# RMSNorm with ReLU on one core: twelve transfers instead of seventeen, and constant addresses on VectorE and ScalarE

## The chip, the core and the metric

The kernel runs on one core of a Trainium2 chip. A core has five engines. Three of them matter here: ScalarE (ACT in the profile) and VectorE (DVE) compute, and SyncE (SP) issues the transfers between main memory (HBM) and the on-chip memory (SBUF, 128 partitions). GpSimd (POOL) only passes semaphores on. TensorE is idle. The transfers themselves are done by 16 DMA engines, each with its own queue. The metric is the device time of one execution in microseconds (us); the time of the kernel before is 160.51 us, the median of three runs that lie between 160.47 and 160.72.

## The reference

```python
def reference(x, gamma, eps):          # x: 16 x 1024 x 512 float32
    rms = np.sqrt(np.mean(x ** 2, axis=-1, keepdims=True) + eps)
    x_norm = x / rms * gamma
    return np.maximum(x_norm, 0).astype(np.float32)
```

Each of the 16,384 rows of 512 numbers is divided by its own root mean square, multiplied by `gamma`, and clamped at zero. The input is 33.55 MB and so is the output, so 67.1 MB pass through the DMA engines whatever the program does.

## The kernel before

**Tiling.** Each partition holds 128 rows in all. They are cut into eight chunks of K = 16 rows (4 MB over all partitions), and each chunk into two groups of G = 8 rows. SBUF has room for six chunks at a time: `slots` is one tensor of six slots, and chunk i lives in slot i % 6. In HBM a chunk is one block of 4 MB in which every partition owns 16 consecutive rows, 32 KB. All computing is done in place in `slots`.

**Transfers.** All are issued by SP, in one written order, and each DMA engine works its queue in that order. There are 17: chunk 0 is loaded in two halves (lines 59 and 77), the others whole, and each of the eight chunks is stored whole (line 87). The two halves are issued ahead of Tile's closing barrier (`tc.close()`, line 97), everything else behind it. The loads of chunks 1 to 5 follow at once. Then SP waits:

```python
    nc.sync.wait_ge(tick3, 6)
    store(0)
    store(1)
    for s in range(2):
        nc.sync.wait_ge(sem_slot[s], 32)
        load(7 + s)
    nc.sync.wait_ge(tick1, 11)
    for i in range(2, nchunks):
        store(i)
```

`tick3` reaches 6 when VectorE has done three rows of group 5 (chunk 2, row 10), `tick1` reaches 11 with the first row of group 10. `load(7 + s)` is chunk 6 + s, which goes into the slot that store s has emptied. Each store also waits until its own chunk is done (`done`).

**ScalarE** (lines 131 to 143) runs a loop over the 16 groups. When GpSimd has told it that a group is there (`ready`), it squares and sums each of the 8 rows (line 136: one ACTIVATE and one read of the accumulator), then takes the root over the 8 sums (line 142) and raises `sq`. **VectorE** (lines 147 to 167) runs a loop over the same groups: a reciprocal of the 8 roots (line 152), one SCALAR_TENSOR_TENSOR for each row that multiplies by the reciprocal and by `gamma` (line 157), and one TENSOR_SCALAR that clamps the whole group, 128x4096 (line 167). Both loops compute the address of each row in a register while they run: ahead of each row's instruction stands a register instruction (FUSED_REGOPS).

**Start.** VectorE clears `gseed` and `eps_sb` (lines 122, 123); ScalarE waits for that, loads `gamma` into four partitions of `gseed` (line 126), and VectorE spreads it over all partitions (line 146).

Of the kernel before, what the change touches and what calls it, by code (L numbers as in the profile page):

```python
# [1 line left out]

# [4 lines left out]

F32 = mybir.dt.float32
ALU = mybir.AluOpType
ACTF = mybir.ActivationFunctionType  # L10


@with_exitstack
def kernel(
    ctx: ExitStack,
    tc: tile.TileContext,
    x: bass.AP,
    gamma: bass.AP,
    eps: bass.AP,
    out: bass.AP,  # L20
):

    nc = tc.nc
    P = nc.NUM_PARTITIONS

    x2 = x.flatten_outer_dims()
    out2 = out.flatten_outer_dims()  # L30
    n, d = x2.shape
    rows = n // P
    inv_d = 1.0 / d
    K = 16
    G = 8
    nchunks = rows // K
    nslots = 6
    ngroups = rows // G
    per = K // G
    xv = x2.rearrange("(c p k) d -> c p k d", p=P, k=K)  # L40
    ov = out2.rearrange("(c p k) d -> c p k d", p=P, k=K)

    def sbuf(name, shape):
        return nc.alloc_sbuf_tensor(name, shape, F32).ap()

    gseed = sbuf("gseed", [P, d])
    gamma_sb = sbuf("gamma_sb", [P, d])
    eps_sb = sbuf("eps_sb", [P, 1])
    ss = sbuf("ss", [P, rows])
    rms = sbuf("rms", [P, rows])  # L50
    rstd = sbuf("rstd", [P, rows])
    slots = sbuf("slots", [P, nslots * K * d])
    junk = nc.alloc_psum_tensor("junk", [P, G, d], F32).ap()


    loads = [(0, 0, G), (0, G, K - G)] + [(i, 0, K) for i in range(1, nchunks)]


    sem_half = nc.alloc_semaphore("half")
    sem_slot = [nc.alloc_semaphore(f"slot{s}") for s in range(nslots)]  # L60
    sem_g = nc.alloc_semaphore("gam")
    sem_z = nc.alloc_semaphore("zero")
    ready = nc.alloc_semaphore("ready")
    sq = nc.alloc_semaphore("sq")
    tick1 = nc.alloc_semaphore("tick1")
    tick3 = nc.alloc_semaphore("tick3")
    done = nc.alloc_semaphore("done")
    sa = nc.alloc_semaphore("sa")
    sv = nc.alloc_semaphore("sv")

    def slot_ap(i):
        s = (i % nslots) * K * d
        return slots[:, s:s + K * d].rearrange("p (k d) -> p k d", d=d)

    def load(m):
        i, a, r = loads[m]
        return nc.sync.dma_start(out=slot_ap(i)[:, a:a + r, :],
                                 in_=xv[i][:, a:a + r, :]
                                 ).then_inc(sem_half if m == 0 else sem_slot[i % nslots], 16)

    def take(engine, sem, n):
        engine.wait_ge(sem, n)
        engine.sem_inc(sem, -n)  # L83

    def store(i):
        nc.sync.wait_ge(done, per * (i + 1))
        nc.sync.dma_start(out=ov[i], in_=slot_ap(i)).then_inc(sem_slot[i % nslots], 16)

    ctx.enter_context(tc.manual_schedule(engines={mybir.EngineType.SP}))
    early = 2
    for m in range(early):
        t = load(m)
        tc.no_tile_sem_insts.add(t.ins.name)
    ctx.close()
    tc.close()
    tc.compile()  # L98

    for m, (i, a, r) in enumerate(loads):  # L100
        if m >= early and i < nslots:
            load(m)


    nc.sync.wait_ge(tick3, 6)
    store(0)
    store(1)
    for s in range(2):
        nc.sync.wait_ge(sem_slot[s], 32)
        load(7 + s)  # L110
    nc.sync.wait_ge(tick1, 11)
    for i in range(2, nchunks):
        store(i)

    for m, (i, a, r) in enumerate(loads):
        if m == 0:
            take(nc.gpsimd, sem_half, 16)
        else:
            nc.gpsimd.wait_ge(sem_slot[i % nslots], 32 * (i // nslots) + 16)
        nc.gpsimd.sem_inc(ready, r // G)  # L120

    nc.vector.memset(gseed, 0.0).then_inc(sem_z, 1)  # L122
    nc.vector.memset(eps_sb, eps).then_inc(sem_z, 1)  # L123

    nc.scalar.wait_ge(sem_z, 1)
    nc.scalar.dma_start(out=gseed[0:P:32, :],
                        in_=gamma[None, :].to_broadcast([P // 32, d])
                        ).then_inc(sem_g, 16)
    nc.scalar.preload_act_table(ACTF.Sqrt)  # L129
    take(nc.scalar, sem_z, 2)  # L130
    with nc.scalar.Fori(0, ngroups) as gi:
        take(nc.scalar, ready, 1)
        base = nc.scalar.snap((gi % (nslots * per)) * (G * d))
        col = nc.scalar.snap(gi * G)
        for j in range(G):
            a = nc.scalar.activation(  # L136
                out=junk[:, j, :], in_=slots[:, bass.ds(base + j * d, d)],
                func=ACTF.Square, accum_out=ss[:, bass.ds(col + j, 1)])
            if j == G - 1:
                a.then_inc(sa, 1)  # L140
        take(nc.scalar, sa, 1)
        nc.scalar.activation(out=rms[:, bass.ds(col, G)], in_=ss[:, bass.ds(col, G)],  # L142
                             func=ACTF.Sqrt, bias=eps_sb, scale=inv_d).then_inc(sq, 1)

    take(nc.vector, sem_g, 16)
    nc.vector.stream_shuffle(gamma_sb, gseed, [0] * 32)  # L146
    with nc.vector.Fori(0, ngroups) as gi:
        take(nc.vector, sq, 1)
        base = nc.vector.snap((gi % (nslots * per)) * (G * d))
        col = nc.vector.snap(gi * G)  # L150
        blk = slots[:, bass.ds(base, G * d)]
        nc.vector.reciprocal(out=rstd[:, bass.ds(col, G)],  # L152
                             in_=rms[:, bass.ds(col, G)]).then_inc(sv, 1)
        take(nc.vector, sv, 1)
        for j in range(G):
            row = slots[:, bass.ds(base + j * d, d)]
            r = nc.vector.scalar_tensor_tensor(  # L157
                out=row, in0=row, scalar=rstd[:, bass.ds(col + j, 1)], in1=gamma_sb,
                op0=ALU.mult, op1=ALU.mult)
            if j == 0:  # L160
                r.then_inc(tick1, 1)
            if j == 2:
                r.then_inc(tick3, 1)
            if j == G - 1:
                r.then_inc(sv, 1)
        take(nc.vector, sv, 1)
        nc.vector.tensor_scalar_max(out=blk, in0=blk, scalar1=0.0).then_inc(done, 1)  # L167

    take(nc.sync, done, ngroups)
    take(nc.sync, tick1, ngroups)  # L170
    take(nc.sync, tick3, ngroups)
    for i in range(nchunks - nslots, nchunks):
        take(nc.sync, sem_slot[i % nslots], 32 * (i // nslots + 1))


# [1 line left out]
_INS = ['x', 'gamma', 'eps']  # L177
_OUTS = [((16, 1024, 512), 'float32')]

_NUMBERS = {'eps': 9.999999747378752e-06}  # L180


# [26 lines left out]
```

## Time and profile before

| what | value |
|---|---|
| median of three runs | 160.51 us (160.47 to 160.72) |
| the profiled execution: its own time | 160.59 us |
| its span, first to last instruction | 159.3 us |
| DMA packets' time, share of 16 engines over the span | 98.2% |
| moved | 67.12 MB, mean 421 GB/s |
| VectorE busy | 126.0 us (79%) |
| ScalarE busy | 86.3 us (54%) |

The span is measured inside the program; 1.3 us of the execution's own time lie outside it. "Busy" counts an engine's compute instructions; register, branch and semaphore instructions are not in it. The DMA share is the time that the packets of a queue took, over 16 engines and the whole span. A packet here is what one DMA engine moves for one partition of one transfer; beside the data packets each engine writes the transfer's semaphore once, as a packet of 4 bytes.

### The profile page before, as it was taken

To read this page: it belongs to the slowest core of one execution; us is meant where nothing else is said; L and a number is where in the kernel's file an instruction comes from. 1 tells how busy PE (TensorE), PEld (TensorE's weight loads), DVE (VectorE), ACT (ScalarE), POOL (GpSimd) and SP (SyncE) were. 2 spreads that over 40 slices of the span, in tenths; PEclk is the share of its full clock that TensorE was granted. 3 is DMA by queue.
4 is the path that set the end of the run, shared out by engine and by line. 5 is a ranking of instruction groups with operands and counts; after the bars stand their busy time and mean duration, and the time that the engine had idled before them with its cause. 6 is when DMAs were issued, how large, how long until landed. Compare 5 with 4: busy or idle time off the path is not lost. (4 is left out here: it accounts for less than half of the span.)

```text
span 159.3 us, 999 instructions
## 1 busy us (share of the span) xinstructions
DVE 126.0 (79%) x164; ACT 86.3 (54%) x273; POOL 0.2 (0%) x4
## 2 busy tenths in 40 slices
DVE  1012989898999999999999999999999989897000
ACT  0388929889989988988920098898500000000000
POOL 0000000000000000000000000000000000000000
DMA  6999999999999999999999999999999999999995
GB/s 193 405 453 424 502 395 395 502 420 395 453 469 395 395 502 420 395 428 494 395 395 444 461 411 395 486 436 395 453 453 403 411 494 411 403 461 453 395 420 247
DMA packets 2456, 67.12 MB, mean 421 GB/s; under 512 B 276, under 2 KB 276, under 8 KB 280
## 3 DMA queue, kind: packets, MB, share of 16 engines
q1 hardware_dynamic: 2448, 67.11, 98.2%
q10 hardware_dynamic: 8, 0.01, 0.0%
HBM read 33.56 MB, written 33.55 MB: 421 GB/s over the span
## 5 line engine op out<-in xcount | busy, mean ns | idle before, releaser
L157 DVE SCALAR_TENSOR_TENSOR slots<-slots,rstd,gamma_sb 128x512 f32 x128 | 86.2, 747 | 4.8 <-DVEq L83 4.8
L136 ACT ACTIVATE junk<-slots 128x512 f32 x128 | 74.4, 581 | 20.6 <-ACTq L83 20.3
L167 DVE TENSOR_SCALAR slots<-slots x16 | 36.7, 2294 | 2.4 <-DVEq L83 0.2
L136 ACT ACTIVATION_READ_ACCUMULATOR junk<-slots x128 | 23.9, 187 | 0.0
L152 DVE RECIPROCAL rstd<-rms x16 | 3.1, 197 | 5.3 <-DVEq L83 5.3
L142 ACT ACTIVATE rms<-ss,eps_sb x16 | 4.8, 301 | 3.0 <-ACTq L83 3.0
L146 DVE LOAD_MASK_SELECT gamma_sb<-gseed x1 | 0.0, 14 | 5.4 <-DVEq L83 5.4
L129 ACT ACT_TABLE_LOAD x1 | 1.3, 1283 | 4.2 <-issue 4.2
L122 DVE MEMSET gseed<- 128x512 f32 x1 | 0.5, 485 | 2.6 <-PEq L98 2.6
L146 DVE STREAM_SHUFFLE gamma_sb<-gseed 128x512 f32<-128x512 f32 x1 | 0.7, 723 | 0.0
L190 POOL MEMSET const-bfloat16-1.0<- 128x1 bf16 x1 | 0.1, 102 | 0.0
L190 POOL MEMSET const-uint8-127<- 128x1 uint8 x1 | 0.1, 102 | 0.0
L190 POOL MEMSET const-float32-0.0<- 128x1 f32 x1 | 0.1, 99 | 0.2 <-issue 0.2
L190 POOL MEMSET const-float32-1.0<- 128x1 f32 x1 | 0.1, 99 | 0.0
L123 DVE MEMSET eps_sb<- 128x1 f32 x1 | 0.1, 59 | 0.0
## 6 DMA issues: line engine op xcount, KB each, us to landing
out_dram<-slots SPq DMA_DIRECT2D x8, 4096.0 KB, 20.6
slots<-in_x_dram SPq DMA_DIRECT2D x7, 4096.0 KB, 29.7
slots<-in_x_dram SPq DMA_DIRECT2D x2, 2048.0 KB, 9.7
gseed<-in_gamma_dram ACTq DMA_DIRECT2D x1, 8.0 KB
```

The costliest lines, as they stand in the source:

```text
L122: nc.vector.memset(gseed, 0.0).then_inc(sem_z, 1)
L123: nc.vector.memset(eps_sb, eps).then_inc(sem_z, 1)
L129: nc.scalar.preload_act_table(ACTF.Sqrt)
L136: a = nc.scalar.activation(out=junk[:, j, :], in_=slots[:, bass.ds(base + j * d, d)], func=ACTF.Square, accum_out=ss[:, bass.ds(col + j, 1)])
L142: nc.scalar.activation(out=rms[:, bass.ds(col, G)], in_=ss[:, bass.ds(col, G)], func=ACTF.Sqrt, bias=eps_sb, scale=inv_d).then_inc(sq, 1)
L146: nc.vector.stream_shuffle(gamma_sb, gseed, [0] * 32)
L152: nc.vector.reciprocal(out=rstd[:, bass.ds(col, G)], in_=rms[:, bass.ds(col, G)]).then_inc(sv, 1)
L157: r = nc.vector.scalar_tensor_tensor(out=row, in0=row, scalar=rstd[:, bass.ds(col + j, 1)], in1=gamma_sb, op0=ALU.mult, op1=ALU.mult)
L167: nc.vector.tensor_scalar_max(out=blk, in0=blk, scalar1=0.0).then_inc(done, 1)
L190: nc = _bacc.Bacc("TRN2", target_bir_lowering=False, num_devices=1)
```

## The change

The announced words are: twelve transfers, six of them with 64 KB descriptors, and VectorE and ScalarE on constant addresses behind Tile's closing barrier. The list in the code has twelve transfers, of which four have 32 rows for each partition, which is 64 KB, and eight have 16 rows, 32 KB; the text goes by the code.

**Transfers.** HBM is now divided into blocks of B = 32 rows for each partition (8 MB), and a transfer moves 16 or 32 rows of such a block. The loads are 16, 16, 32, 32, 16 and 16 rows, the stores the same. A 16-row transfer takes 32 KB out of every 64 KB of HBM. Each transfer has its own semaphore. The first load is a whole chunk, so nothing can start on half a chunk. The first store waits for row 10 of chunk 2 as before (`tick`), the store of chunks 2 and 3 waits for chunk 4 to be done (`done` 5).

**VectorE** has its body written out once for each chunk with fixed addresses. A loop runs it twice: chunks 0 to 5, and then chunks 6 and 7 in the code of chunks 0 and 1. Chunks 0, 1, 2, 6 and 7 take a reciprocal for each group, chunks 3, 4 and 5 one for the whole chunk, for which they wait for both groups. The clamp is one instruction for the chunk, 128x8192, behind all its rows. **ScalarE** keeps its loop with register addresses for groups 0 to 9, 12 and 13, and has fixed addresses and one root for the whole chunk in chunks 5 and 7. Both engines get an `addr_align` ahead of the barrier, which places the code behind it at slot 128 of a block of 256 instructions. **GpSimd** clears `gseed` and `eps_sb`.

```diff
-    loads = [(0, 0, G), (0, G, K - G)] + [(i, 0, K) for i in range(1, nchunks)]
+    B = 2 * K
+    xv = x2.rearrange("(c p k) d -> c p k d", p=P, k=B)      # ov likewise
+    order = [(L, 0, 16), (L, 16, 16), (L, 32, 32), (L, 64, 32),
+             (S, 0, 16), (S, 16, 16), (L, 96, 16), (L, 112, 16),
+             (S, 32, 32), (S, 64, 32), (S, 96, 16), (S, 112, 16)]
+    def transfer(m):
+        kind, a, r = order[m]
+        here = slots[:, a % room * d:(a % room + r) * d].rearrange("p (k d) -> p k d", d=d)
+        there = (ov if kind == S else xv)[a // B, :, a % B:a % B + r, :]
+        ends = (there, here) if kind == S else (here, there)
+        return nc.sync.dma_start(out=ends[0], in_=ends[1]).then_inc(sems[m], 16)
...
+    for engine in (nc.scalar, nc.vector):
+        engine.addr_align(256, offset=128, max_nops=0)
...
+        if (kind, a) == (S, 0):
+            nc.sync.wait_ge(tick, 1)
+        elif (kind, a) == (S, 32):
+            nc.sync.wait_ge(done, 5)
+        if kind == S:
+            nc.sync.wait_ge(done, (a + r) // K)
+        elif a >= room:
+            take(nc.sync, sems[order.index((S, a - room, r))], 16)
+        transfer(m)
...
-    nc.vector.memset(gseed, 0.0).then_inc(sem_z, 1)
-    nc.vector.memset(eps_sb, eps).then_inc(sem_z, 1)
+    nc.gpsimd.memset(gseed, 0.0).then_inc(sem_z, 1)
+    nc.gpsimd.memset(eps_sb, eps).then_inc(sem_z, 1)
...
+    def chunk_sums(i):
+        c = (i % nslots) * K
+        take(nc.scalar, ready, per)
+        for j in range(K):
+            a = square((c + j) * d, c + j, j % G)
+            if j % G == G - 1:
+                a.then_inc(sa, 1)
+                nc.scalar.wait_ge(sa, (j + 1) // G)
+        root(c, K).then_inc(sq, per)
+        nc.scalar.sem_inc(sa, -per)
+    with nc.scalar.Fori(0, 2) as o:
+        with nc.scalar.Fori(o * 12, o * 4 + 10) as gi:
...
+        with nc.scalar.If_lt(nc.scalar.to_reg(o), 1):
+            chunk_sums(5)
+        with nc.scalar.Else():
+            chunk_sums(7)
...
+    def factors(c, r, n):
+        nc.vector.wait_ge(sq, n)
+        nc.vector.reciprocal(out=rstd[:, c:c + r], in_=rms[:, c:c + r]).then_inc(sv, 1)
...
+    def clamp(c, r):
+        blk = slots[:, c * d:(c + r) * d]
+        return nc.vector.tensor_scalar_max(out=blk, in0=blk, scalar1=0.0)
+    def chunk_rows(s, by_group=False, clamps=(K,), ticked=None):
+        c = s * K
+        for j in range(K):
+            if by_group and j % G == 0:
+                factors(c + j, G, (c + j) // G + 1)
+            elif j == 0:
+                factors(c, K, per * (s + 1))
+            row = slots[:, (c + j) * d:(c + j + 1) * d]
+            r = nc.vector.scalar_tensor_tensor(
+                out=row, in0=row, scalar=rstd[:, c + j:c + j + 1], in1=gamma_sb,
+                op0=ALU.mult, op1=ALU.mult)
...
+                b = clamp(c + j + 1 - n, n)
+        b.then_inc(done, 1)
+    with nc.vector.Fori(0, 2) as o:
+        chunk_rows(0, by_group=True)
+        chunk_rows(1, by_group=True)
+        with nc.vector.If_lt(nc.vector.to_reg(o), 1):
+            chunk_rows(2, by_group=True, ticked=10)
+            chunk_rows(3)
+            chunk_rows(4)
+            chunk_rows(5)
...
```

## The prediction

> **What bounds the kernel now.** I read the page first: busy times, the slices, the queues.
>
> ```profile
> DVE 126.0 (79%) x164; ACT 86.3 (54%) x273; POOL 0.2 (0%) x4
> ...
> DMA  6999999999999999999999999999999999999995
> ...
> q1 hardware_dynamic: 2448, 67.11, 98.2%
> ```
>
> No compute engine fills the span, but the 16 DMA engines do: every slice but the first and the last is full, and SP's queue alone is at 98.2%. The bytes do not change, so only three things can move the end: the time that these bytes take, the start and the tail, and a moment at which the queue runs dry. The windows by stage say whether it does (columns: stretch, its length, busy us of DVE, ACT, POOL, clock, DMA share, GB/s).
>
> ```profile
> 0.00:14.00 14.00, 1.23 (x4) 6.36 (x18) 0.20 (x4) 1.00 0.92 375
> 14.00:62.00 48.00, 44.83 (x60) 41.62 (x133) 0.00 (x0) 1.00 1.00 431
> 62.00:82.00 20.00, 18.81 (x24) 17.04 (x56) 0.00 (x0) 1.00 1.02 434
> 82.00:101.00 19.00, 18.11 (x25) 9.34 (x30) 0.00 (x0) 1.00 0.99 428
> 101.00:147.00 46.00, 43.07 (x54) 11.90 (x39) 0.00 (x0) 1.00 1.00 433
> ```
>
> It never does. VectorE is close behind, and its timeline gives its pace (start, duration):
>
> ```profile
> 20.53 2.29 DVE L167 TENSOR_SCALAR slots<-slots  x1 [0.16 <-DVEq L83]
> 22.74 0.20 DVE L152 RECIPROCAL rstd<-rms  x1
> 23.23 5.39 DVE L157 SCALAR_TENSOR_TENSOR slots<-slots,rstd,gamma_sb 128x512 f32 x8 [0.30 <-DVEq L83]
> 28.77 2.29 DVE L167 TENSOR_SCALAR slots<-slots  x1
> ```
>
> A group takes 28.77-20.53 = 8.24 us, a chunk 16.48. From the first reciprocal at 14.48 it never waits for data: 14.48 + 16 x 8.24 = 146.3. Then the tail:
>
> ```profile
> 144.15 2.29 DVE L167 TENSOR_SCALAR slots<-slots  x1
> 146.47 0.33 SPq L87 DMA_DIRECT2D out_dram<-slots  x1
> ```
>
> The last store is issued at 146.47. The first issue of the program (0.73) has its first packet at 1.75, so an issue needs 1.0 us. By the trace's packet records the earliest DMA engine finishes the store before at 147.99: 0.5 us to spare. So the kernel is bound by DMA, with VectorE half a microsecond from taking over. The chain of waits itself shows nothing useful here: it holds only the last clamp.
>
> **What the skill says.** (1) DMA: Bandwidth & Descriptors, "Where 436 GB/s comes from": a ceiling of 435 GB/s from 16 ports. The trace agrees: 431 to 434 in the full windows. No larger descriptor can bring much. (2) The same page, "Latency and other measured facts", HBM row pitch: copies whose partitions lie 512 KiB apart run at 207 GB/s instead of 214. The change doubles our pitch from 32 to 64 KB, for which neither page nor trace has a figure. (3) VectorE: DVE Perf Modes, "Mode 2x_2P": fp32 with one source runs two elements a cycle; its formula gives (151 + 4096/2)/0.96 = 2,291 ns, the trace 2,294. (4) Runtime: NRT & Kernel Launch, "Instruction fetch mechanics": code is fetched in blocks of 256 instructions, two are held, and a taken branch out of them waits for a transfer. No fetch shows inside the span of before.
>
> **DMA time.** From the packet records, the median engine takes 4.862 us for a 2 MB transfer (8 packets and a semaphore write) and 9.681 for an undisturbed one of 4 MB. Two halves cost 9.724, so joining two transfers saves 0.043 (6 ns of it the semaphore write; 4.6 ns per packet saved). If doubling again saves as much: 17 to 12 transfers is five joinings, 0.21 us. Bounds: if 64 KB went out as two packets of 32, the four large joinings would save only their semaphore write, 0.07 in all; by the packets' own durations (611 against 1,213 ns, 9 ns for each of 40 packets, 5 writes of 9 ns) it would be 0.41. I take the pitch, since packets overlap by some ns.
>
> The tail holds one thing more. In the last store 15 engines end between 157.67 and 158.18, one at 158.75. Almost every packet of one engine is 5 to 50 ns long in the stores from 61 to 78 and 100 to 148, while ScalarE works or VectorE changes groups, and no engine is alone in this during the loads. It looks tied to how many instructions run; the change removes 144 of VectorE's register instructions and a quarter of ScalarE's. At most 0.57 can come back; my estimate is 0.1, since ScalarE keeps three quarters of its loop.
>
> **Start.** First load 4 MB instead of 2. Both halves together landed at 13.03 (semaphore records); the whole will at 12.98. From landing to ScalarE's first row was 8.73-8.29 = 0.45, from there to the reciprocal 14.48-8.73 = 5.75; fixed addresses and a wait joined to its instruction save about 0.15 (the 76 ns register instruction and its gap). VectorE starts at 12.98+0.45+5.75-0.15 = 19.0, which is 4.5 later. `gamma` landed at 8.31, right behind the first transfer (8.29); it will land at 13 and be spread by 14, 5 us ahead. GpSimd's 128x512 memset has no row: between VectorE's 0.49 and, as an estimate, four times that; nothing needs it before 12. The jump to slot 128 delays the barrier by very little, and 8 MB are queued ahead of it.
>
> **VectorE's new pace.** Rows start every 0.662 us in the records, and the register instructions run beside them: fixed addresses gain nothing there. They gain between reciprocal and first row (0.49 to about 0.30), and before the clamp (0.24 extra to 0.20). The clamp of 8,192, with (3), takes 4.42, or 4.34 to the next start, against two of 2.21. A chunk: 2 x (0.30+5.30)+0.20+4.34 = 15.74 with two reciprocals, 15.44 with one, instead of 16.48. With 0.2 of wait for group 1 and 0.3 for the loop's branch, chunks end at 34.9, 50.7, 66.4, 81.9, 97.3, 112.7, 128.8 and 144.5. So it ends 2 us earlier than now despite the later start.
>
> **Is it fed?** ScalarE's groups take 5.78. Chunk 2 now waits for 8 MB: landing 42.1, root for VectorE 48.1, needed 50.7. Chunk 3 waits for both its groups: 42.5 + 3 x 5.78 + 5.6 = 65.4, needed 66.4. Both fit.
>
> **Is SP's queue fed?** Earliest engine dry, against issue plus 1.0. First store: row 10 of chunk 2 ends at 50.7+5.6+0.3+1.3+0.75 = 58.7, packet at 59.7; dry at 60.68-0.13 = 60.5: 0.8 to spare. Stores of chunks 2 and 3: chunk 4 ends 97.3, packet 98.4; dry at 99.58-0.13 = 99.4: 1.0. Those of 4 and 5, and of 6: over 5 us. Last store: 145.6 against 147.99-0.21 = 147.8: 2.2. Loads 6 and 7 wait for stores 0 and 1 as now, behind one transfer in the queue.
>
> **The sum.** Profiled execution 160.59 - 0.21 - 0.1 = 160.28. The median runs 0.08 under it: **160.2 us**. About 0.2%, 0.32 us, is what a measurement of this kernel can tell from no change; the forecast lies at that edge.
>
> **Rivals.**
> *The late engine vanishes (faster).* 0.21 + 0.57: 159.7. For it: its delays come where instructions are many. Against: ScalarE's loop remains in most groups.
> *VectorE comes late (slower).* Place: the stores of chunks 2 and 3. If a chunk still took 16.48, chunk 4 would end at 101.4 and the queue be dry for 3 us; the last chunk would end near 151.4, and the time be 164.8. It decides from 1.0 us of delay at chunk 4, 0.2 for each chunk. For it: the start really is 4.5 later. Against: the clamp's formula fits the row to 3 ns. An instruction fetch at the loop's back edge (about 113) would act on the last store alone, beyond 2.2 us.
> *The 64 KB pitch slows HBM.* Loads of chunks 3 and 4 took 9.70 to 9.71 instead of 9.681. If the pitch adds 0.03 for every 4 MB, 16 x 0.03 = 0.5: 160.7. At 3%, as at 512 KiB, the loss would be 5 us.
> *The joining does nothing*: 64 KB cut in two, 160.5.
>
> **How the numbers follow.** The forecast with its spread of 159.8 to 160.5: 0.66 (it falls on both sides of 160.19: 0.30 faster, 0.36 same). The late engine vanishes: 0.08, faster. VectorE late or a fetch stall: 0.13, slower. Pitch: 0.09, of which 0.06 slower. Nothing: 0.04, same. That makes 0.38 faster, 0.43 same, 0.19 slower. The range from 159.6 to 161.1 leaves out most of the VectorE case and the far end of the pitch.
>
> **What would show it.** 512 packets of 64 KB at about 2,414 ns pitch, 1,728 packets on SP's queue; DMA full in every window from 14 to 147; VectorE's first reciprocal near 19.0, its clamp near 4.42, its end near 144.5; the first store issued near 58.8, the third near 97.5. Wrong if a store's issue comes after the queue has run dry, if packets of 64 KB exceed 2,430 ns, or if the late engine's tail grows.

## The result: slower by one per cent

The changed kernel takes 162.24 us (median of four runs, 161.87 to 162.56) against 160.62 us for the kernel before in the same series. The ratio is 1.0097, with a 95% interval of 1.0069 to 1.0125 (all ratios here are estimated over the single executions, so they differ a little from the quotient of the medians). It was forecast at 160.2, with a range from 159.6 to 161.1. The profiled execution took 162.56 us, its span is 160.9.

### The profile after

First the page of the changed kernel: busy times, the DMA line of the slices, the queues, and three groups of instructions (busy us, mean ns of one, idle time ahead).

```profile
DVE 123.9 (77%) x151; ACT 85.7 (53%) x271; POOL 0.8 (0%) x6
...
DMA  6999999979969969999999999999999999899993
...
q1 hardware_dynamic: 1728, 67.11, 97.6%
q14 instruction: 3, 0.02, 0.0%
...
L187 DVE SCALAR_TENSOR_TENSOR slots<-slots,rstd,gamma_sb 128x512 f32<-128x512 f32 x128 | 86.0, 746 | 0.5
...
L176 DVE TENSOR_SCALAR slots<-slots 128x8192 f32<-128x8192 f32 x8 | 35.4, 4426 | 0.3
L169 DVE RECIPROCAL rstd<-rms 128x8 f32<-128x8 f32 (+1 forms) x13 | 2.7, 208 | 9.0 <-ACT rms L134 9.0
```

VectorE does the same rows and needs 2 us less, and its clamps are 4,426 ns long. Of the 9.0 us that it waited ahead of reciprocals, 8.84 lie ahead of the first. SP's queue moved the same bytes in 1,728 packets. New is queue 14: packets that fetch instructions, none of which stood in the span of the kernel before. The sixes and sevens in the DMA line are where packets of 64 KB straddle slices, not gaps: the windows of the changed kernel (columns as before) show DMA full from 14 to 147 us.

```profile
0.00:14.00 14.00, 0.72 (x2) 1.28 (x1) 0.76 (x6) 1.00 0.90 372
14.00:62.00 48.00, 41.67 (x56) 38.41 (x123) 0.00 (x0) 1.00 1.01 435
62.00:82.00 20.00, 19.90 (x20) 18.79 (x61) 0.00 (x0) 1.00 0.98 406
82.00:101.00 19.00, 18.89 (x25) 14.18 (x47) 0.00 (x0) 1.00 1.04 438
101.00:147.00 46.00, 42.69 (x51) 13.04 (x42) 0.00 (x0) 1.00 0.99 430
```

The engines are busy all the time and yet move less in places: 406 GB/s from 62 to 82 us, where the kernel before had 434. A part of that difference is counting, since a packet counts whole in the window in which it starts (the DMA share there is 0.98 against 1.02); over 14 to 147 us it is 429 against 432 GB/s. Time has gone into longer packets, not into waiting. VectorE's timeline of the changed kernel (start, duration) shows that this is not for want of finished chunks:

```profile
19.85 0.20 DVE L169 RECIPROCAL rstd<-rms 128x8 f32<-128x8 f32 x1 [8.84 <-ACT rms L134]
20.09 5.39 DVE L187 SCALAR_TENSOR_TENSOR slots<-slots,rstd,gamma_sb 128x512 f32<-128x512 f32 x8
25.68 0.20 DVE L169 RECIPROCAL rstd<-rms 128x8 f32<-128x8 f32 x1 [0.20 <-ACT rms L134]
...
31.34 4.43 DVE L176 TENSOR_SCALAR slots<-slots 128x8192 f32<-128x8192 f32 x1
...
93.10 4.43 DVE L176 TENSOR_SCALAR slots<-slots 128x8192 f32<-128x8192 f32 x1
...
139.51 4.43 DVE L176 TENSOR_SCALAR slots<-slots 128x8192 f32<-128x8192 f32 x1
```

It starts 5.4 us later than before, at 19.85, and its last clamp ends at 143.9, 2.5 us earlier than before.

### Where the time went

Each DMA engine writes a transfer's semaphore when it has finished its part. The median engine is the median of the 16 ends of a transfer; the last engine is the one that ends it, and the lag is the time between the two. From these records, the difference between the two profiled executions, 162.56 - 160.59 = 1.97 us, is the sum of four parts:

| part | before | after | difference |
|---|---|---|---|
| end of the median engine | 157.87 | 158.72 | +0.85 |
| last engine behind the median | 0.88 | 1.81 | +0.93 |
| from the last packet to the end of the span | 0.51 | 0.37 | -0.14 |
| own time outside the span | 1.33 | 1.66 | +0.33 |

*The median engine* loses where the direction changes. It takes 10.35 us for the second store (9.90 before), 10.00 and 9.99 for the loads of chunks 6 and 7 (9.70 and 9.69): +0.45, +0.30, +0.29. All other stretches together give 0.19 back, which is the joining of transfers. A 32 KB packet takes 1,213 ns when nothing disturbs it; near 80 us packets of 1,560 to 2,230 ns stand on most engines, near 100 us packets of 1,320 to 2,220 ns.

*The last engine* is late from the start: in the first load one engine ends at 13.38 and one at 13.05, the others by 12.42. Two instruction packets of 8 KB are in the records at 2.71 and 3.97 us. The lag stays, grows by 0.5 us at the change near 60 us, where one load packet of 64 KB takes 2,994 ns instead of 2,418, and is largest from the change near 100 us on.

*Outside the span*: a third instruction packet stands at 162.30, behind the span's end.

### The profile page after: what moved, and what is told of

It is laid out like the page before. It is cut to its first block, busy times and chain, and to the rows that moved or that the text cites. A ratio compares the mean times of both kernels' runs of the same rounds, so it can differ in the third digit from the quotient of the medians.

```text
span 160.9 us, 711 instructions
## 1 busy us (share of the span) xinstructions
DVE 123.9 (77%) x151; ACT 85.7 (53%) x271; POOL 0.8 (0%) x6
## 3 DMA queue, kind: packets, MB, share of 16 engines
q1 hardware_dynamic: 1728, 67.11, 97.6%
## 4 chain that ended last, share of the span: by engine, by line
DVE 68%; issue 6%; ACT 0%; DVEq 0%; ACTq 0%
DVE slots L187 50%; DVE slots L176 17%; DVE rstd L169 1%; ACT rms L134 0%; DVEq L201 0%; ACTq L134 0%; DVEq L211 0%
## 5 line engine op out<-in xcount | busy, mean ns | idle before, releaser
L187 DVE SCALAR_TENSOR_TENSOR slots<-slots,rstd,gamma_sb 128x512 f32<-128x512 f32 x128 | 86.0, 746 | 0.5
L130 ACT ACTIVATE junk<-slots 128x512 f32 (+1 forms) x128 | 74.4, 581 | 21.4 <-ACTq L84 21.1
L176 DVE TENSOR_SCALAR slots<-slots 128x8192 f32<-128x8192 f32 x8 | 35.4, 4426 | 0.3
L130 ACT ACTIVATION_READ_ACCUMULATOR junk<-slots (+1 forms) x128 | 23.9, 187 | 0.0
L169 DVE RECIPROCAL rstd<-rms 128x8 f32<-128x8 f32 (+1 forms) x13 | 2.7, 208 | 9.0 <-ACT rms L134 9.0
L134 ACT ACTIVATE rms<-ss,eps_sb (+1 forms) x14 | 4.2, 302 | 2.4 <-ACTq L84 2.2
L115 POOL MEMSET gseed<- 128x512 f32 x1 | 0.5, 524 | 1.9 <-POOLq L98 1.9
```

The costliest lines, as they stand in the source:

```text
L115: nc.gpsimd.memset(gseed, 0.0).then_inc(sem_z, 1)
L130: return nc.scalar.activation(out=junk[:, j, :], in_=slots[:, bass.ds(row, d)], func=ACTF.Square, accum_out=ss[:, bass.ds(col, 1)])
L134: return nc.scalar.activation(out=rms[:, bass.ds(col, r)], in_=ss[:, bass.ds(col, r)], func=ACTF.Sqrt, bias=eps_sb, scale=inv_d)
L169: nc.vector.reciprocal(out=rstd[:, c:c + r], in_=rms[:, c:c + r]).then_inc(sv, 1)
L176: return nc.vector.tensor_scalar_max(out=blk, in0=blk, scalar1=0.0)
L187: r = nc.vector.scalar_tensor_tensor(out=row, in0=row, scalar=rstd[:, c + j:c + j + 1], in1=gamma_sb, op0=ALU.mult, op1=ALU.mult)
```

## The experiments

Three changes of direction matter below: from the loads to store 0 (near 60 us), from store 1 to load 6 (near 80), and from load 7 to store 2 (near 100; "store 2" is the store of chunks 2 and 3 where these are joined). "Excess" is the time of all packets that start from 57 to 63, 76 to 88 or 96 to 104 us over 611, 1,213 or 2,418 ns for 16, 32 or 64 KB, divided by 16 engines. Ratios are to the kernel before in the same series.

### Which part of the change costs the time

**1. The changed kernel without `addr_align`.**

```diff
-    for engine in (nc.scalar, nc.vector):
-        engine.addr_align(256, offset=128, max_nops=0)
```

> The changed kernel without the two address alignments; all else as changed. Fetch theory: the jump to slot 128 makes ScalarE and VectorE fetch instructions at 2.7 and 4.0 us, through two of the 16 DMA engines, which are late by 0.7 and 1.0 us from the first transfer on; without it those packets and the late engines go, and the time falls from 162.2 to about 161.0. Pitch theory: the loss comes where stores and loads meet (79 to 82 and 98 to 101 us), from HBM rows 64 KB apart; then the time stays near 162.2.

162.49 us, 1.0122 (1.0101 to 1.0144). The fetches do not go away, they move: instruction packets at 50.92 and 82.62, none at the start or the end. Leaving the alignment out gives nothing back. The fetches are not cleared by that, since the account is another: in this trace the median engine ends only 0.27 later than before, but the last one is 2.69 behind it. While the packet at 50.92 runs, for 309 ns, 15 data packets are under way instead of 16, and the data packet that starts when it ends takes 3,044 ns instead of 2,418. So this fetch made one DMA engine about 0.9 us late.

**2. The kernel before with both `addr_align`** (and with the two engines in `manual_schedule`, as in the changed kernel).

```diff
...
+    for engine in (nc.scalar, nc.vector):
+        engine.addr_align(256, offset=128, max_nops=0)
```

> The kernel before with only the two address alignments added. Fetch theory: instruction packets inside the span and one or two late engines, 161.6 to 161.9 instead of 160.6. Pitch theory: 160.6, no change.

160.75 us, 1.0014 (1.0001 to 1.0027), with instruction packets at 1.79 and 3.85. A seventh of the loss, only just clear of nothing.

**3. The kernel before with blocks of 64 KB in HBM** (each transfer takes 32 KB out of every 64).

```diff
-    xv = x2.rearrange("(c p k) d -> c p k d", p=P, k=K)
+    xv = [x2.rearrange("(c p k) d -> c p k d", p=P, k=2 * K)[i // 2, :, i % 2 * K:i % 2 * K + K, :]
+          for i in range(nchunks)]
...
```

> The kernel before with only the layout in HBM changed: each 16-row transfer takes 32 KB out of every 64 KB, still 17 transfers and no packet over 32 KB. Pitch theory: packets grow where store 1 and load 6 meet, 161.4 or more. Fetch theory: 160.6, no change.

160.62 us, 1.0005 (0.9995 to 1.0014). The pitch, the distance in HBM from one partition's rows to the next one's, costs nothing that can be told from no change.

**4. The changed kernel with blocks of 32 KB**: the same twelve transfers, all packets 32 KB.

```diff
-    B = 2 * K
+    B = K
...
```

> The changed kernel with the old layout in HBM (32 KB of each partition in a 4 MB block); its four 32-row transfers carry two packets of 32 KB for each partition. Pitch theory: the median engine gets its 0.85 us back, about 161.3. Fetch theory: the late engines stay, 162.0 to 162.4. If the single packets of 64 KB are what hurts, this run gains like the pitch theory says while the run before with the new layout shows no loss.

161.41 us, 1.0044 (1.0031 to 1.0057). About half of the loss is gone. Since 3 shows that the pitch is free, and 5 that packets of 64 KB are, both beside the compute of before, this is no price of either by itself, but beside the changed compute they count; the excess at the three changes is 0.03, 0.23 and 0.13 here, against 0.06, 0.81 and 0.35 in the changed kernel.

**5. The kernel before with joined transfers**: load of chunks 4 and 5, stores of 2 and 3 and of 4 and 5, in the blocks of 64 KB; 14 transfers, compute and ticks as before.

```diff
...
-    for i in range(2, nchunks):
-        store(i)
+    store(2, 2)
+    store(4, 2)
+    store(6)
+    store(7)
...
```

> The kernel before, computing as it did, with three of the four joined transfers in single packets of 64 KB (load of chunks 4 and 5, stores of 2 and 3, and of 4 and 5) and the new layout in HBM; 14 transfers, no alignment. Packet theory: the last load packets ahead of a 64 KB store are long on all engines (0.3 to 0.7 us each), so 161.0 to 161.4. Late-engine theory: without an engine that an instruction packet has made late nothing happens, 160.4 to 160.6.

160.46 us, 0.9988 (0.9981 to 0.9995). Joining is worth 0.15 us. (Its profile fell on an outlying execution of 161.34 and isn't used for an account. Near 60 it has an excess of 0.29, with store 0 issued 3.4 us ahead of the end of the loads, the excess not counted.)

**6. The same with packets of 32 KB.**

```diff
-    xb = x2.rearrange("(c p k) d -> c p k d", p=P, k=2 * K)
+    xb = x2.rearrange("(c p k) d -> c p k d", p=P, k=K)
...
```

> The same three joined transfers with the old layout, in two packets of 32 KB for each partition. Both theories: no loss, 160.4 to 160.6, of which three joinings account for a gain of at most 0.13.

160.58 us, 1.0001 (0.9993 to 1.0010). The gain of 5 isn't seen with packets of 32 KB; the two intervals just touch.

**7. Number 5 with both `addr_align`.**

```diff
...
+    for engine in (nc.scalar, nc.vector):
+        engine.addr_align(256, offset=128, max_nops=0)
```

> The kernel with three joined transfers of 64 KB packets, plus the two address alignments, which put two instruction packets into the first 4 us. Packet theory: as without the alignments plus the 0.14% that these cost alone, 161.2 to 161.6. Late-engine theory: the late engine is held up further at each change from loads to stores, 161.3 or more, while the kernel without the alignments stays near 160.5.

160.49 us, 0.9995 (0.9986 to 1.0003).

**8. The changed kernel's compute with the 17 transfers of before.**

```diff
-    B = 2 * K
+    B = K
...
-    order = [(L, 0, 16), (L, 16, 16), (L, 32, 32), (L, 64, 32),
+    order = ([(L, 0, 8), (L, 8, 8)] + [(L, a, 16) for a in range(16, 96, 16)] +
...
```

> The changed kernel with the transfers and the layout of before: 17, chunk 0 in two halves. Constant addresses, whole-chunk clamps, GpSimd's memsets and the alignments stay. If the compute side carries part of the loss (instruction packets, and one at the end outside the span), 161.0 to 161.4; if the transfers carry all of it, 160.6.

162.46 us, 1.0109 (1.0092 to 1.0126). As much as the whole loss, without a single joined transfer. Together with 3, 5 and 7 this says: the new transfers cost nothing beside the compute of before, and the new compute of VectorE and ScalarE is enough for such a loss. It isn't the same loss, though. Here the excess is 0.82, 0.10 and 0.47 at the three changes, in the changed kernel 0.06, 0.81 and 0.35, and number 4 shows that the transfers count beside the new compute. What the compute sets for the queue is the moment at which stores may be issued. Number 8 issues its stores 4.8 us earlier than the changed kernel, since chunk 0 starts on a half. Its SP timeline:

```profile
54.27 0.83 SPq L80 DMA_DIRECT2D out_dram<-slots  x2
73.66 10.01 SPq L80 DMA_DIRECT2D slots<-in_x_dram  x2
92.73 15.68 SPq L80 DMA_DIRECT2D out_dram<-slots  x4
```

Stores 0 and 1 go out at 54.27, store 2 at 92.73; in the kernel before, by the same view, it is 58.30 and 98.19:

```profile
58.30 0.82 SPq L87 DMA_DIRECT2D out_dram<-slots  x2
71.23 10.35 SPq L77 DMA_DIRECT2D slots<-in_x_dram  x2
98.19 15.65 SPq L87 DMA_DIRECT2D out_dram<-slots  x4
```

In number 8 the last load packet of every one of the 16 engines, at 59.4 to 59.9 us, is 350 to 1,043 ns too long, and 15 of them are again too long by 219 to 648 ns at 97.6 to 98.7. Hence the next theory: a store that is in the queue well ahead of the loads' end makes their last packets longer.

### When a store is issued

**9. The kernel before without its two waits for ticks.**

```diff
-    nc.sync.wait_ge(tick3, 6)
...
-    nc.sync.wait_ge(tick1, 11)
```

> The kernel before without its two waits on the ticks: store 0 is issued as soon as its chunk is done (31 us instead of 58.3), store 2 right behind load 7 (near 82 instead of 98.2). Early-store theory: a store that lies in the queue while an engine still works on its last load packets makes these long; 0.6 to 0.9 us at each of the two changes from loads to stores, 161.6 to 162.4. Rival, that it is not the issue but the compute work of the changed kernel running beside the changes: 160.6, no change, since the compute side is the same and the queue never runs dry.

161.17 us, 1.0034 (1.0019 to 1.0048). SP's timeline:

```profile
30.93 16.83 SPq L87 DMA_DIRECT2D out_dram<-slots  x2
71.80 10.30 SPq L77 DMA_DIRECT2D slots<-in_x_dram  x2
82.15 64.49 SPq L87 DMA_DIRECT2D out_dram<-slots  x6
```

Store 0 went out at 30.93, and the load packets at 58.2 to 60.2 are 108 to 591 ns longer: an excess of 0.71. But store 2 went out at 82.15, 18 us ahead of the end of the loads, and there the excess is 0.01. The theory holds for one change and fails for the other.

**10. The changed kernel with a later store 2**: it waits for the first row of chunk 5.

```diff
-            nc.sync.wait_ge(done, 5)
+            nc.sync.wait_ge(tick, 2)
...
-            chunk_rows(5)
+            chunk_rows(5, ticked=0)
...
```

> The changed kernel with one wait moved: the store of chunks 2 and 3 waits for row 0 of chunk 5 (98.5 us) instead of the end of chunk 4 (97.55). Early-store theory: the 0.35 us per engine near 98 to 101 go, and the late engines lose less, 161.3 to 161.8. Rival: 162.2 as before.

161.40 us, 1.0049 (1.0032 to 1.0066). SP's timeline of the changed kernel, and then that of this one:

```profile
59.09 0.82 SPq L80 DMA_DIRECT2D out_dram<-slots  x2
72.46 10.02 SPq L80 DMA_DIRECT2D slots<-in_x_dram  x2
97.55 15.69 SPq L80 DMA_DIRECT2D out_dram<-slots  x2
...
58.88 0.82 SPq L80 DMA_DIRECT2D out_dram<-slots  x2
72.51 10.01 SPq L80 DMA_DIRECT2D slots<-in_x_dram  x2
98.29 14.74 SPq L80 DMA_DIRECT2D out_dram<-slots  x2
```

Moving one issue from 97.55 to 98.29 gave 0.84 us back, half of the loss. The excess there fell from 0.35 to 0.05. The first row of chunk 5 is the point in VectorE's work at which the kernel before lets this store go (`tick1` 11): the change had moved the wait up to the end of chunk 4, and this run moves it back.

**11. Number 8 with both stores late**, at 57.78 and 98.38. For the first, chunk 2's clamp is cut in two and the tick comes from row 12.

```diff
-            chunk_rows(2, by_group=True, ticked=10)
+            chunk_rows(2, by_group=True, clamps=(G, K), ticked=12)
...
-            chunk_rows(5)
+            chunk_rows(5, ticked=7)
...
```

> The changed compute side with the 17 transfers of before, but the two stores that follow loads issued as late as in the kernel before: store 0 at about 58.1 instead of 54.3 (the clamp of chunk 2 is cut in two, and the tick comes from row 12), store 2 at about 98.5 instead of 92.7 (row 7 of chunk 5). Early-store theory: the 0.82 and 0.47 us per engine at the two changes go, from 162.46 to about 161.0; what is left is the instruction packet ahead of the end (0.35) and one late engine. Rival, the compute side itself: 162.3 to 162.6.

161.22 us, 1.0037 (1.0022 to 1.0051): 1.24 of 1.85 us are back. The excess is 0.10, 0.14 and 0.00 instead of 0.82, 0.10 and 0.47.

**12. The kernel before with store 0 issued 1.4 us earlier.**

```diff
-    nc.sync.wait_ge(tick3, 6)
+    nc.sync.wait_ge(tick1, 6)
```

> The kernel before with store 0 waiting for the first row of group 5 (near 56.9 us) instead of its third (58.3). The queue runs dry at 60.7, an engine's last load packet begins near 59.5. Early-store theory: 0.4 to 0.8 us per engine between 57 and 62, 161.0 to 161.4; 160.6 if nothing depends on a microsecond.

161.15 us, 1.0036 (1.0024 to 1.0047). SP's timeline:

```profile
56.87 0.83 SPq L87 DMA_DIRECT2D out_dram<-slots  x2
71.93 10.15 SPq L77 DMA_DIRECT2D slots<-in_x_dram  x2
98.08 15.65 SPq L87 DMA_DIRECT2D out_dram<-slots  x4
```

Nothing else was changed, and 1.4 us cost as much as the 27 us of number 9. The long packets start from 58.2 us on, and the first engine ends its last load only at 61.33, so they are long before any engine comes to the store's own packets. The last load ahead of the store takes the median engine 10.41 us instead of 9.71, and the windows of this run show it as missing rate, with the engines fully busy (426 where the kernel before has 431, over 48 us):

```profile
14.00:62.00 48.00, 44.94 (x60) 41.60 (x135) 0.00 (x0) 1.00 1.00 426
```

This is the plainest of the runs: the tick of the kernel before doesn't only keep a store from coming too late; it keeps it from coming too early.

**13 and 14. The kernel before with an earlier store 2**, at 96.80 and at 88.55.

```diff
-    nc.sync.wait_ge(tick1, 11)
+    nc.sync.wait_ge(done, 10)
```

Number 14 waits for 9 in the place of 10.

> The kernel before with one wait changed: store 2 waits for group 9 to be done (near 97.0 us) instead of the first row of group 10 (98.2). The queue runs dry at 99.6. If the harm starts as soon as the store lies in the queue before an engine takes its last load packet (near 98.4), about 0.3 to 0.5 us per engine at this change, 160.9 to 161.1; if only the whole earliness of several us counts, 160.6.

160.65 us, 1.0008 (0.9998 to 1.0018).

> The kernel before with store 2 waiting for group 8 (near 88.7 us). If every early store costs, 0.5 to 0.8 us per engine as for store 0 issued at 31 us, 161.1 to 161.4; if a store issued far ahead of this change is free, as in the run without both ticks, where store 2 went out at 82.2 and no packet near 98 was long, 160.6.

160.81 us, 1.0018 (1.0009 to 1.0028). The profile is of its fastest execution (160.40). Load 7 takes the median engine 10.00 us instead of 9.69. The sign is that of the theory, the size half of that at store 0.

The two changes from load to store, sorted by lead (the median engine's end of the load, less the excess, minus the issue of the store):

| change | kernel | lead, us | excess, us per engine |
|---|---|---|---|
| near 60 | changed | 1.6 | 0.06 |
| | before | 2.5 | 0.02 |
| | 1 | 2.6 | 0.24 |
| | 13 | 2.7 | 0.04 |
| | 11 | 3.0 | 0.10 |
| | 12 | 4.0 | 0.70 |
| | 8 | 6.5 | 0.82 |
| | 9 | 29.9 | 0.71 |
| near 100 | 11 | 1.3 | 0.00 |
| | before | 1.6 | 0.01 |
| | 10 | 2.0 | 0.05 |
| | 4 | 2.3 | 0.13 |
| | changed | 2.8 | 0.35 |
| | 13 | 2.9 | 0.08 |
| | 1 | 3.1 | 0.58 |
| | 8 | 7.7 | 0.47 |
| | 14 | 11.2 | 0.35 |
| | 9 | 18.1 | 0.01 |

With a lead up to 2.3 us the excess is at most 0.13, with one of 4 us and more it is 0.35 to 0.82, except in number 9. Between them it is anything from 0.02 to 0.58.

### The late engine, and the change near 80 us

**15. Number 10 with store 0 one row later**, at 59.55.

```diff
-            chunk_rows(2, by_group=True, ticked=10)
+            chunk_rows(2, by_group=True, ticked=11)
```

> The changed kernel with the later wait for the store of chunks 2 and 3, and store 0 one row later too (59.6 instead of 58.9 us), for the late engine, which takes its last load packet at 59.1. Late-engine theory: its packet, 835 ns too long in the run with the one later wait, loses most of that, and the time falls from 161.4 to 160.9 to 161.2. Rival: the queue runs dry on the other engines for 0.1 to 0.3 us, 161.5 to 161.7.

161.68 us (160.91 to 163.02 in 16 executions), 1.0083 (1.0056 to 1.0110). No gain. The executions fall in two groups, nine from 160.9 to 161.7 and seven from 162.5 to 163.0. The profile is of the upper group: one engine is 2.16 us behind the median at the end, most of it from one packet at 81.16 that took 2,641 ns and one at 99.52 that took 1,755. One thing the later store 0 did do: the lag didn't grow at the change near 60 (0.87 ahead of it and 0.89 behind it), where it grew in the traces of the changed kernel and of 10, 17 and 18, to 1.46 to 1.77. For an engine that is a microsecond late, the lead of a store is a microsecond longer. But the lag came back at the two later changes.

**16. Number 5 with load 6 held back to 77.1 us** (row 6 of group 7); without the wait it goes out as soon as store 0 has emptied its slot.

```diff
...
+        if s == 0:
+            nc.sync.wait_ge(tick7, 8)
...
```

> The kernel with three joined transfers of 64 KB (160.46) with load 6 held back until row 6 of group 7 is done (77.5 us instead of 71.3), short of the end of store 1 at 80.1. If a load that lies in the queue behind a store does the same harm, the 0.13 to 0.2 us per engine at this change shrink: 160.2 to 160.35. If only stores behind loads do it: 160.46, no change.

160.36 us, 0.9986 (0.9978 to 0.9994). It has the lowest median of all, 0.14% under the kernel before and 1.9 us under the changed one, and can't be told from number 5 (0.9988). The delay itself did little: the excess near 80 is 0.16, within the 0.13 to 0.23 of most other runs. So here load 6 doesn't harm the stores ahead of it by being issued early.

**17. Number 10 once more**, as a control on the chip of number 18.

> The same program as the changed kernel with its late third store (store of chunks 2 and 3 at row 0 of chunk 5), as the control for the next run. Its first series gave 161.27 to 161.52 in four executions and 162.35 in one; with store 0 one row later 16 executions fell into two groups, 161.0 to 161.7 and 162.5 to 163.0. Theory (the change from store 1 to load 6 at 78.5 to 83 us costs up to 0.9 us per engine in some executions and 0.2 in others): again 161.0 to 161.7, with some executions near 162.5. Rival (the two groups came from the later store 0): all within 161.2 to 161.6.

161.39 us, 1.0053 (1.0033 to 1.0072), executions from 161.13 to 162.19. The excess near 80 is 0.94, in an execution of 161.13.

**18. Number 10 with chunk 3's clamp cut in two**, so that less of it falls on the change near 80.

```diff
-            chunk_rows(3)
+            chunk_rows(3, clamps=(11, K))
```

> As the control, but VectorE clamps chunk 3 in two parts, rows 0 to 10 at about 74.5 to 77.6 us and rows 11 to 15 at about 81 to 82.5, instead of all 16 rows at 77.5 to 82.0. Theory (the long clamp meets the packets at which the DMA engines go from store 1 to load 6, 78.5 to 81 us, and makes them longer): that excess falls from 0.9 to 0.25 us per engine or less, no execution is near 162.5, and the median is 160.7 to 161.1. Rival (the clamp has no part in it): the excess stays between 0.2 and 0.9 and the times are those of the control, 161.0 to 161.7 with some near 162.5.

161.64 us, 1.0056 (1.0039 to 1.0073). VectorE's timeline shows the clamp moved:

```profile
74.31 3.09 DVE L176 TENSOR_SCALAR slots<-slots 128x5632 f32<-128x5632 f32 x1
77.32 3.39 DVE L187 SCALAR_TENSOR_TENSOR slots<-slots,rstd,gamma_sb 128x512 f32<-128x512 f32 x5
80.75 1.49 DVE L176 TENSOR_SCALAR slots<-slots 128x2560 f32<-128x2560 f32 x1
```

The packets from 78.5 to 79.1 us are as long as in the control, with no clamp running: the excess is 0.93. My theory that the long clamp makes them so has fallen.

### The accounts of the profiled executions

The same four parts as above, each as the difference from the kernel before, in us. Their sum is the difference of the execution's own time.

| kernel | median engine | last engine's lag | last packet to span's end | outside the span | sum |
|---|---|---|---|---|---|
| changed | +0.85 | +0.93 | -0.14 | +0.33 | +1.97 |
| 1, no align | +0.27 | +1.81 | -0.14 | -0.02 | +1.92 |
| 4, 32 KB | -0.01 | +0.67 | -0.15 | +0.35 | +0.86 |
| 8, 17 transfers | +1.16 | +1.02 | -0.16 | +0.17 | +2.19 |
| 11, 8 with late stores | -0.06 | +0.34 | -0.14 | +0.15 | +0.29 |
| 10, late store 2 | +0.61 | +1.03 | -0.15 | +0.27 | +1.76 |
| 17, the same again | +0.56 | +0.11 | -0.14 | +0.01 | +0.54 |
| 18 | +0.61 | +0.47 | -0.13 | +0.34 | +1.29 |
| 15 | +0.46 | +1.28 | -0.14 | +0.35 | +1.95 |
| 12, before, store 0 early | +0.53 | +0.06 | 0.00 | -0.01 | +0.58 |

10 and 17 are the same program: its executions differ by the late engine and by what lies outside the span. The executions of number 10 other than the profiled one took 161.27 to 161.52.

### What is settled and what is open

*Shown.* Store 0 issued 1.4 us earlier, 4.0 instead of 2.5 us ahead of the end of the loads, costs 0.6 us in the kernel before, with nothing else changed (12). In the changed kernel, issuing store 2 0.74 us later gives 0.84 back (10; 17, the same on another chip, has 1.0053). Number 15, with the same late store 2 and a later store 0, doesn't keep that gain (1.0083): nine of its 16 executions lie with those of 10, and the other seven with or above those of the changed kernel. Beside the compute of before, joining, packets of 64 KB and the pitch of 64 KB are free or a small gain (3, 5, 16), and the alignment costs 0.22 us (2); in number 5 it costs 0.1, with intervals that overlap (7 against 5, 0.9995 against 0.9988).

*Read from traces, not isolated by a run.* An instruction packet after the span goes with 1.48 to 1.68 us outside it (seven traces), none with 1.31 to 1.34 (the thirteen others): 0.15 to 0.35 us. The fetches at the start go with a first load in which the last engine is about a microsecond late (13.38 and 12.29 in the changed kernel, 7.72 and 7.48 before): 0.73 to 1.17 us behind the median in the ten traces that have them, 0.13 to 0.28 in the ten that don't.

*Open.* Why number 9 pays nothing near 100 us. Why the changed kernel and 10, 15, 17 and 18 have an excess of 0.8 to 0.9 near 80 and all others 0.01 to 0.23: it takes the packets of 64 KB and the alignment together (4 and 1 lack one of them), but number 7 has both and 0.16. The clamp isn't the cause (18). The issue of load 6 isn't either as far as the traces show: it goes out at 72.46 in the changed kernel and at 72.62 in 1, whose excess is 0.10 (16 held it back only in a kernel without the large excess). A busy ScalarE isn't, since it is busy for 4.97 of the 5 us from 78 in 1 and 4 as well as in 10. And why the lag of one engine differs by a microsecond between executions of one program. So of the 1.6 us lost, half comes back with the later store 2, of which the median engine shows 0.24 to 0.29 (10 and 17 against the changed kernel) and the rest isn't traced; the other half is spread over the fetches, the late engine and the change near 80, in shares that these runs do not separate.

## Why the prediction was wrong

**Joining: right.** Predicted -0.21. The median engine takes 9.66 us for 4 MB in packets of 64 KB (19.32 for 8), as the 2,414 ns of pitch said; the stretches without a change of direction gave back 0.19. But the term priced every packet at its undisturbed pitch. On the median engine the changes of direction took 1.04 us more than before (0.75 near 80, 0.29 near 100), and for that the working had no term.

**Start: late by 0.85.** VectorE's first reciprocal came at 19.85, not 19.0. From ScalarE's first row (14.33) it took 5.52 us, as predicted (5.60). The rest is the landing: the working took 12.98 for it by the semaphore records, and by the same records it came at 13.85, behind the late engine. `gamma` and the memset (524 ns) did no harm.

**VectorE's pace: right, and a little too slow.** The clamp took 4,426 ns (4.42 predicted, by a formula whose 151 cycles the page that the prediction names states for fp32 `tensor_tensor`; the prediction carried them over to two elements a cycle). Chunk 4 ended at 97.5 (97.3), the last at 143.9 (144.5). That chunk 4 was so close is in part luck: a start 0.85 us late against chunks of about 15.54 and 15.35 us instead of 15.74 and 15.44. After its start it waited for ScalarE only the predicted 0.2 us, for group 1.

**"Is SP's queue fed?": the step that failed.** Its numbers were right: the first store was predicted near 58.8 and issued at 59.09, the third near 97.5 and issued at 97.55, and no queue ran dry. Wrong was the reading: it held an issue only against the moment at which the queue would run dry, so an issue ahead of need cost nothing. "0.8 to spare" and "1.0" are margins against that end alone. Number 12 shows that the other end has a price too, and number 10 that 0.74 us at store 2 are worth 0.84 of the 1.62 lost; the rest of the loss isn't explained by this step. In the kernel before both stores are issued only 2.5 and 1.6 us ahead of the loads' end, though chunk 0 was finished by 30.9 and chunk 2 by 82.2 (number 9); what that is worth the trace of before alone did not show, and no step of the working asked.

**The tail of the late engine: wrong sign.** I took it for something that instructions cause and put in -0.1; it became +0.93. In the changed kernel the lag is 1.09 us after the first load, 1.66 at the end of the load near 60, 0.99 near 80 and 1.81 near 100, and stays there; it no longer grows in the stores, as it did before.

**The instruction fetch: missed.** The text says that a fetch at the loop's back edge "would act on the last store alone"; no instruction packet stands there. It looked at the engine that waits for the code, and not at the transfer that brings it. The Trainium skill, Runtime: NRT & Kernel Launch, "Instruction fetch mechanics", calls the cost of crossing from one block of instructions to the next mostly hidden. In this case 8 KB packets at 2.71 and 3.97 us take 0.31 us each of the DMA engines, which are the bound, and one follows the span.

**The rivals.** VectorE did not come late, and the case with 164.8 us had the store in the wrong place: too late instead of too early. The 64 KB pitch costs nothing (3); the loads of 9.70 to 9.71 us that spoke for it are those of chunks 4 and 5 in the records, not 3 and 4. Against "the joining does nothing" stand the 19.32 us for 8 MB, and 5. The late engine did not vanish. The range ended at 161.1, since no case in it let a transfer become longer because of what stands behind it in the queue.

## What to carry to other kernels

In a kernel bound by DMA, a store behind loads can be issued too early: here a lead of 1.3 to 2.3 us over the end of the loads cost at most 0.13 us, and one of 4 us and more mostly cost 0.35 to 0.8 us. What a store issued too late would cost no run here shows. So a change that moves the compute engine's schedule, or the wait of a store, must look at the issue times of the stores, even where each still comes in time. Joining transfers into packets of 64 KB with the ticks as they were (number 5) is a small gain, 0.12%.

## What the runs showed of the hardware

- A store in the queue made the load packets ahead of it longer: by 0.7 us per engine in 12, where it was issued 4.0 us ahead of their end, though not near 100 in 9, with 18.1 us. The Trainium skill, DMA: Bandwidth & Descriptors, "Two DMAs through the same engine are not ordered", says that an engine pipelines descriptors and has separate queues for reads and writes. That a store's reads run beside the last writes of a load would fit; these traces do not show reads and writes apart, so it is only argued.
- The reverse change, a load behind a store, does not go by the lead: 0.16 us with load 6 held to 77.1, 0.13 to 0.22 in the kernel before and its close variants where it is issued at about 71 to 72, apart from the outlying execution of number 5 (0.02) and those of the next point.
- Where the first change cost 0.7 us or more (8, 9, 12), the change near 80 cost only 0.01 to 0.10.
- Doubling the pitch of partitions in HBM from 32 to 64 KB had no effect that can be told from none (1.0005, 0.9995 to 1.0014).
- Instruction packets of 8 KB take time from the data: while the one at 50.92 us of number 1 ran, 15 data packets were under way instead of 16, and the next one took 3,044 ns instead of 2,418. They take 0.3 to 0.6 us, the first at the start up to 1.4 us.
